# Low halves of split weights: an accumulating DMA in place of a VectorE subtraction

## The chip, the cores and the metric

The kernel runs on one core of a Trainium2 chip. The metric is device time in microseconds (us) of one execution. The engines are TensorE (PE; PEld is its weight load), VectorE (DVE), ScalarE (ACT), GpSimd (POOL) and SyncE (SP). Each works through its own instructions in order; they wait for each other and for DMAs through semaphores.

## The reference

One decoder layer on a 1024 x 1024 float32 input. Behind a projection to seven parts stand two token mixers in parallel and an output projection:

```python
h = rms_norm(x, pre_g)
conv_in, z_c, u_s, z_s, g_c, g_s = split(h @ w_in)
ca, cb = split(conv_in)
cu = silu(layer_norm(causal_depthwise_conv(ca * sigmoid(cb), conv_w, conv_b)))
conv_out = (cu * silu(z_c)) @ w_conv_out
y = gelu(s5_mimo(u_s, ...))                      # complex-diagonal state, 32 groups
y = y * sigmoid(y @ w_glu + b_glu)
ssm_out = (y * silu(z_s)) @ w_ssm_out
merged = sigmoid(g_c) * conv_out + sigmoid(g_s) * ssm_out
out = x + rms_norm(merged @ w_out, post_g)
```

## The kernel before

**Three passes for each product.** TensorE works on a rounded format (fp32r). To keep float32 precision, both factors of a product are split into a high half, the rounded value, and a low half, the value minus its high half. A product then has three passes: high weight with high data, high weight with low data, low weight with high data. The weights of one output tile of 128 channels are a *unit*: a 128 x 1024 tile for the products of depth 1024 (cb, ca, gc, zc, gs, zs, co, and us), and 128 x 512 for those of depth 512 (glu, so). A unit of depth 1024 has 8 slices k, each with three passes of two matmuls of 512 columns, 48 matmuls; a unit of depth 512 has 24. The units follow each other in a list, `seq`: first us3, then pairs of cb and ca with gc and zc between them, the four glu, the zs, the alternating gs and so, and at the end the eight co. Then comes the output product, `po`, whose weights (wo) are split too.

**How a weight comes to TensorE.** SP loads the raw tile of a unit (`wr_`, L706). ACT copies it to the rounded high half (`wh_`, L716, in `wsplit_h`). DVE subtracts the high half from the raw tile and writes the low half (`wl_`, L724, in `wsplit_l`). Raw, high and low tiles have two buffers each. During the product of one unit the next unit is split. After the low half is made, `wload` asks for the raw tile of the unit two further on, into the raw buffer that has just been read. That load therefore waits on SP's queue until the raw tile has been read, and what SP is to issue later waits behind it.

**Where the split stands in the program.** `product` issues the matmuls slice by slice. For a unit of depth 1024 it calls `flush` after slice 1, which issues the eviction of the product before (ACT or DVE reads the PSUM tile), `wsplit_h` after slice 2 and `wsplit_l` after slice 4. For a unit of depth 512 the places are slice 0, slice 0 and slice 2. The buffers, not these places alone, decide when the split can run: the high and low tile of unit u+1 use the buffers of unit u-1, and are free when TensorE has finished with u-1.

**Other work.** The S5 mixer (parameters, then four quarters), the depthwise convolution (some 350 multiply-adds on DVE, L551) and the layer norm are generators. `clk.tick` places their instructions between the matmuls, by a running model of when DVE is free; `clk.fg` adds to it what other work costs DVE. POOL has little: sums of squares at the start, powers in small pieces for the S5 parameters (L234), a memset in each S5 quarter (L462), and powers for the norms. SP issues all DMAs.

Of the kernel before, what the change touches and what calls it, by code (L numbers as in the profile page):

```python
# [10 lines left out]
AF = mybir.ActivationFunctionType  # L11
ALU = mybir.AluOpType
# [23 lines left out]
def tile_hybrid_block(  # L36
# [25 lines left out]
    V, A, G, PE = nc.vector, nc.scalar, nc.gpsimd, nc.tensor  # L62
# [17 lines left out]
    def PS(name, tag):  # L80
        return ps.tile([128, 1024], F32, tag=tag, name=name)

    def f32(t):
        return t.bitcast(F32)
# [599 lines left out]
    clk = Clock()  # L684
# [6 lines left out]
    def wsrc(kind, m):  # L691
        base = {"cb": M_CB, "ca": M_CA, "gc": M_GC, "gs": M_GS, "zc": M_ZC, "zs": M_ZS, "us": M_US}
        if kind in base:
            return w_in[base[kind] + m], 8
        return {"glu": (w_glu, 4), "so": (w_so, 4), "co": (w_co, 8), "wo": (w_out, 8)}[kind][0][m], \
            {"glu": 4, "so": 4, "co": 8, "wo": 8}[kind]
# [3 lines left out]
    def wload():  # L700
        if rnext[0] < len(order):
            u = order[rnext[0]]
            rnext[0] += 1
            src, kt = wsrc(*u)
            raw = wp.tile([128, 1024], F32, tag="wraw", name=f"wr_{u[0]}{u[1]}", bufs=WRAW)
            nc.sync.dma_start(out=raw[:, 0:kt * 128], in_=src)  # L706
            raws[u] = (raw, kt)

    def wsplit_h():
        if wnext[0] < len(order):  # L710
            u = order[wnext[0]]
            wnext[0] += 1
            raw, kt = raws.pop(u)
            n = kt * 128
            h = wp.tile([128, 1024], F32R, tag="wh", name=f"wh_{u[0]}{u[1]}", bufs=WHL)
            A.activation(out=h[:, 0:n], in_=raw[:, 0:n], func=AF.Copy)  # L716
            half[0] = (u, raw, h, n)

    def wsplit_l():
        if half[0]:  # L720
            u, raw, h, n = half[0]
            half[0] = None
            l = wp.tile([128, 1024], F32R, tag="wl", name=f"wl_{u[0]}{u[1]}", bufs=WHL)
            V.tensor_tensor(out=l[:, 0:n], in0=raw[:, 0:n], in1=f32(h[:, 0:n]), op=ALU.subtract)  # L724
            clk.fg(1.14 * n / 1024)
            wt[u] = (h, l)
            wload()

# [5 lines left out]
    def flush():  # L734
        while posts:
            posts.pop(0)()

    def js(j):
        return slice(j * 512, (j + 1) * 512)

    def product(name, u, rh, rl, tag="mm"):
        p = PS(name, tag)
        h, l = wt.pop(u)
        kt = wsrc(*u)[1]
        for k in range(kt):
            ks = slice(k * 128, (k + 1) * 128)
            for lhs, rhs, st, sp_ in ((h, rh, k == 0, False), (h, rl, False, False), (l, rh, False, k == kt - 1)):
                for j in range(2):
                    PE.matmul(p[:, js(j)], lhsT=lhs[:, ks], rhs=rhs(k, j), start=st, stop=sp_)  # L749
            if kt == 4 and k == 0:  # L750
                wsplit_h()
            if k == (1 if kt == 8 else 0):
                flush()
            if kt == 8 and k == 2:
                wsplit_h()
            if k == (4 if kt == 8 else 2):
                wsplit_l()
            clk.tick(1.296)
        return p

    def proj(u, tag="mm"):
        return product(f"p{u[0]}{u[1]}", u, lambda k, j: xh[:, k, js(j)], lambda k, j: xl[:, k, js(j)], tag)
# [55 lines left out]
    for k in range(8):  # L818
# [19 lines left out]
        h, l = wus[k // 2]  # L838
# [3 lines left out]
        for n_, (m, i) in enumerate([(m, i) for i in range(3) for m in range(3)]):  # L842
            lhs, rhs = passes[i]
            for j in range(2):
                js_ = slice(j * 512, (j + 1) * 512)
                PE.matmul(usp[m][:, js_], lhsT=lhs[:, kk[m]], rhs=rhs[:, k, js_], start=(k == 0 and i == 0),
                          stop=(k == 7 and i == 2))
            if n_ == 4:
                if k == 4:
                    x_sums(rb)  # L850
                if k == 5:
                    rbc = x_spread(rb)
                    clk.dve = max(clk.dve, clk.now + 1.5)
                    clk.add('s5', s5_chain())
                for k_ in {6: (0, 1), 7: (2, 3)}.get(k, ()):
                    x_norm(k_, rbc)
                if k == 7:
                    wsplit_h()
                    wsplit_l()
            clk.tick(0.45)  # L860
# [25 lines left out]
    for u in seq:  # L886
# [29 lines left out]
        elif kind == "yhl":  # L916
            clk.until('s5', lambda: s5_done[0])
            continue
        elif kind == "glu":
            p = product(f"pgl{m}", u, lambda k, j: yh[k][:, js(j)], lambda k, j: yl[k][:, js(j)])  # L920

            def f(p=p, m=m):
# [16 lines left out]
        elif kind == "gs":  # L939
            p = proj(u)  # L940

            def f(p=p, m=m):
                sgs[m] = T(f"gst{m}")
                A.activation(out=sgs[m], in_=p, func=AF.Sigmoid)  # L944
        elif kind == "so":
            p = product(f"pso{m}", u, lambda k, j: y2h[k][:, js(j)], lambda k, j: y2l[k][:, js(j)])

            def f(p=p, m=m):
# [43 lines left out]
    for k in range(8):  # L992
        if k < WHL:
            if ("wo", k) not in wt:
                wsplit_h()
                wsplit_l()
            woh[k], wol[k] = wt[("wo", k)]
        else:
            raw = wp.tile([128, 1024], F32, tag="wraw", name=f"wor{k}", bufs=WRAW)
            nc.sync.dma_start(out=raw, in_=w_out[k])  # L1000
            woh[k], wol[k] = xw[0][:, k, :], xw[1][:, k, :]
            split(woh[k], wol[k], raw)
# [134 lines left out]
```

## Time and profile before

| | us |
|---|---|
| median of 3 runs | 856.16 |
| lowest and highest of the runs | 855.4, 856.76 |
| the profiled execution, its own time | 855.18 |
| its span in the profile | 853.1 |
| PE busy | 826.1 |
| DVE busy | 630.6 |
| ACT busy | 279.3 |
| POOL busy | 45.9 |

The mean granted TensorE clock of the profiled execution was 0.992. How to read the rows: a row of the timeline gives the start, the length, the engine, the line, the operation, what is written and read, the shape, how many instructions were merged, and in brackets the idle time of the engine just before with what ended it. In a row of the groups the two numbers after the bar are the busy time in us and the mean of one instruction in ns. In a row of a DMA the last number is the median time from issue to landing. The ends of matmuls are modelled.

### The profile page before, as it was taken

What the parts mean: (1) busy time and instruction counts of PE and PEld (TensorE: products, weight loads), DVE (VectorE), ACT (ScalarE), POOL (GpSimd) and SP (SyncE); (2) the same over time, 40 slices, a digit from 0 to 9 for tenths busy, and PEclk for the clock granted to TensorE, in tenths of its full rate; (3) what the DMA queues carried; (4) which work ended last, traced back from release to release, by engine and by line L of the source; (5) the groups of instructions that cost most, each with busy time, mean ns of one, the idle gap of its engine ahead of it and who ended that gap; (6) DMA issues with size and microseconds to landing.
All of it is one profiled execution on the core that took longest, in us unless ns stands there. A gap on an engine that the chain in (4) does not pass through costs nothing.

```text
span 853.1 us, 9817 instructions
## 1 busy us (share of the span) xinstructions
PE 826.1 (97%) x3888; PEld 685.6 (80%) x3888; DVE 630.6 (74%) x902; ACT 279.3 (33%) x292; POOL 45.9 (5%) x32
## 2 busy tenths in 40 slices
PE   6898999999999999999999999999999999999996
PEld 5776778888888888888888888888878788888885
DVE  5576699989989988999998959589594544452242
ACT  7233155253344426333222221133252411122121
POOL 3660000000000000000000000000000000000010
PEclk9799999999999999999999999999999999999999
DMA  9103433233231321211111212212253343325142
GB/s 336 51 25 123 149 99 107 80 90 123 91 83 66 110 75 50 75 49 50 50 38 62 87 38 99 74 61 85 103 210 135 117 184 142 142 85 195 49 173 98
DMA packets 34028, 86.58 MB, mean 101 GB/s; under 512 B 8176, under 2 KB 12912, under 8 KB 33984
## 3 DMA queue, kind: packets, MB, share of 16 engines
q1 hardware_dynamic: 33984, 85.97, 29.5%
q8 instruction: 30, 0.49, 0.2%
q14 instruction: 14, 0.11, 0.0%
HBM read 61.71 MB, written 18.87 MB: 94 GB/s over the span
## 4 chain that ended last, share of the span: by engine, by line
PE 81%; DVE 6%; issue 1%; ACT 1%; DMA 1%; SPq 1%; DVEq 0%; POOLq 0%; ACTq 0%
PE pco L749 10%; PE po L1010 10%; PE pgs L749 9%; PE pgc L749 9%; PE pca L749 9%; PE pzc L749 9%; PE pcb L749 9%; PE pzs L749 5%; PE pso L749 4%; PE pgl L749 2%; PE yp L504 1%; PE yp L503 1%; PE ep L425 1%; PE lnp L589 1%; SPq L204 1%
## 5 line engine op out<-in xcount | busy, mean ns | idle before, releaser
L551 DVE SCALAR_TENSOR_TENSOR pp<-ext,cw,pp 128x512 f32<-128x512 f32 x232 | 165.0, 744 | 7.6 <-ACT pp L542 7.6
L551 DVE SCALAR_TENSOR_TENSOR acc<-ext,hs,acc 128x512 f32<-128x512 f32 x120 | 89.3, 744 | 0.0
L1010 PE MATMUL po<-wox,mgh 128*128 128x512 f32 x192 | 52.3, 389 | 0.0
L749 PE MATMUL pcb<-xh,wh_cb 128*128 128x512 f32 x128 | 40.2, 395 | 2.3 <-ACT wh_cb L716 2.3
L1010 PEld LDWEIGHTS po<-wox,mgh 128*128 128x128 f32 x192 | 36.0, 188 | 7.5
L1026 DVE TENSOR_TENSOR o<-po,postg 128x1024 f32<-128x1024 f32 (+1 forms) x9 | 10.0, 1106 | 42.0 <-ACT q L1025 42.0
L749 PE MATMUL pcb<-xh,wl_cb 128*128 128x512 f32 x128 | 39.7, 391 | 1.4 <-DVE wl_cb L724 1.3
L749 PE MATMUL pco<-cuh,wl_co 128*128 128x512 f32 x128 | 39.5, 390 | 1.3 <-DVE wl_co L724 1.3
L749 PE MATMUL pgs<-xh,wh_gs 128*128 128x512 f32 x128 | 39.6, 391 | 1.0 <-ACT gst L944 1.0
L749 PE MATMUL pgc<-xh,wh_gc 128*128 128x512 f32 x128 | 40.2, 395 | 0.0
L749 PE MATMUL pzc<-xh,wh_zc 128*128 128x512 f32 x128 | 40.0, 394 | 0.0
L749 PE MATMUL pca<-xh,wh_ca 128*128 128x512 f32 x128 | 39.8, 392 | 0.0
L749 PE MATMUL pgs<-xh,wl_gs 128*128 128x512 f32 x128 | 39.5, 390 | 0.0
L749 PE MATMUL pgc<-xl,wh_gc 128*128 128x512 f32 x128 | 39.5, 389 | 0.0
L749 PE MATMUL pzc<-xl,wh_zc 128*128 128x512 f32 x128 | 39.5, 389 | 0.0
L749 PE MATMUL pco<-cuh,wh_co 128*128 128x512 f32 x128 | 39.4, 389 | 0.0
L749 PE MATMUL pgc<-xh,wl_gc 128*128 128x512 f32 x128 | 39.4, 389 | 0.0
L749 PE MATMUL pca<-xh,wl_ca 128*128 128x512 f32 x128 | 39.4, 389 | 0.0
L749 PE MATMUL pcb<-xl,wh_cb 128*128 128x512 f32 x128 | 39.4, 389 | 0.0
L749 PE MATMUL pco<-cul,wh_co 128*128 128x512 f32 x128 | 39.4, 389 | 0.0
L749 PE MATMUL pzc<-xh,wl_zc 128*128 128x512 f32 x128 | 39.4, 389 | 0.0
L749 PE MATMUL pca<-xl,wh_ca 128*128 128x512 f32 x128 | 39.4, 389 | 0.0
(270 smaller groups left out, 1784.3 us busy)
## 6 DMA issues: line engine op xcount, KB each, us to landing
xt<-in_xt_dram SPq DMA_DIRECT2D x8, 512.0 KB, 6.1
wr_cb<-in_w_in_dram SPq DMA_DIRECT2D x8, 512.0 KB, 3.2
wr_ca<-in_w_in_dram SPq DMA_DIRECT2D x8, 512.0 KB, 3.3
wr_gc<-in_w_in_dram SPq DMA_DIRECT2D x8, 512.0 KB, 3.5
gc_scratch<-gct SPq DMA_DIRECT2D x8, 512.0 KB, 3.3
wr_zc<-in_w_in_dram SPq DMA_DIRECT2D x8, 512.0 KB, 3.2
zc_scratch<-zct SPq DMA_DIRECT2D x8, 512.0 KB, 2.6
wr_gs<-in_w_in_dram SPq DMA_DIRECT2D x8, 512.0 KB, 3.2
```

The source lines that it names most:

```text
L204: nc.sync.dma_start(out=usU[m][16 * (7 - t):16 * (8 - t)].rearrange("p (g n) -> p g n", g=8), in_=src[t])
L425: pe(lambda g, s: PE.matmul(epp[:, s], lhsT=R[:, s], rhs=U[:, s], start=True, stop=True), 1.8)
L503: PE.matmul(yp[:, s], lhsT=U[:, s], rhs=Mt[:, s], start=True, stop=False)
L504: PE.matmul(yp[:, s], lhsT=Sx[:, s], rhs=O1[:, s], start=False, stop=True)
L551: V.scalar_tensor_tensor(out=o, in0=src(e, r), scalar=w, in1=o, op0=ALU.mult, op1=ALU.add)
L589: PE.transpose(p[:, t * 128:(t + 1) * 128], acc[c][:, t * 128:(t + 1) * 128], ident)
L749: PE.matmul(p[:, js(j)], lhsT=lhs[:, ks], rhs=rhs(k, j), start=st, stop=sp_)
L1010: PE.matmul(p[:, js(j)], lhsT=lhs[k][:, s], rhs=rhs[k][:, js(j)], start=st, stop=sp_)
L1026: V.tensor_tensor(out=o[:, s], in0=p, in1=pog[:, s], op=ALU.mult)
```

## The change

The subtraction on DVE is gone. In its place ACT copies the high half once more, with scale -1, into the low tile, and POOL issues a DMA that reads the raw tile and adds it to the low tile in place: minus high plus raw. The model's charge for DVE goes with it. And both halves are now split after slice 0 of a product, whatever its depth; the next raw load stands there too, ahead of the eviction of the product before.

```diff
             l = wp.tile([128, 1024], F32R, tag="wl", name=f"wl_{u[0]}{u[1]}", bufs=WHL)
-            V.tensor_tensor(out=l[:, 0:n], in0=raw[:, 0:n], in1=f32(h[:, 0:n]), op=ALU.subtract)
-            clk.fg(1.14 * n / 1024)
+            A.activation(out=l[:, 0:n], in_=f32(h[:, 0:n]), func=AF.Copy, scale=-1.0)
+            G.dma_start(out=l[:, 0:n], in_=raw[:, 0:n], accum_op=ALU.add)
             wt[u] = (h, l)
             wload()
...
                 for j in range(2):
                     PE.matmul(p[:, js(j)], lhsT=lhs[:, ks], rhs=rhs(k, j), start=st, stop=sp_)
-            if kt == 4 and k == 0:
+            if k == 0:
                 wsplit_h()
+                wsplit_l()
             if k == (1 if kt == 8 else 0):
                 flush()
-            if kt == 8 and k == 2:
-                wsplit_h()
-            if k == (4 if kt == 8 else 2):
-                wsplit_l()
             clk.tick(1.296)
```

Three places of the order are shown. The first is POOL's queue, from the square root of the mean squares (r8t) over the powers of the S5 parameters (spt) to the first memset of an S5 quarter (Mt). Before:

```order
L165 TENSOR_TENSOR r8t_98<-ssq8_97,mhalf_86 128x8
L234 TENSOR_TENSOR spt1_341<-spar_339,lamt_90 128x8 x4
L234 TENSOR_TENSOR spt4_384<-spar_339,spt3_382 128x8 x4
L462 MEMSET Mt0_966 128x1024
L462 MEMSET Mt1_1369 128x1024
```

And with the change:

```order
L234 TENSOR_TENSOR spt1_341<-spar_339,lamt_90 128x8 x4
L234 TENSOR_TENSOR spt4_384<-spar_339,spt3_382 128x8
L725 DMA wl_us3_396<-wr_us3_309 128x1024
L725 DMA wl_cb0_467<-wr_cb0_311 128x1024
L725 DMA wl_ca0_523<-wr_ca0_399 128x1024
L234 TENSOR_TENSOR spt4_384<-spar_339,spt3_382 128x8 x3
L725 DMA wl_gc0_640<-wr_gc0_470 128x1024
L725 DMA wl_cb1_765<-wr_cb1_526 128x1024
L725 DMA wl_ca1_857<-wr_ca1_643 128x1024
L462 MEMSET Mt0_936 128x1024
```

POOL now issues an accumulating DMA for each unit, in line with its other work; three of the four pieces of the second power stand behind the DMAs of us3, cb0 and ca0.

The second place is ACT's queue where gs and so alternate: the unit gs1 is split during the product of so0 (gst0 is the eviction of gs0, ext5, pp5 and acc5 belong to the convolution). Before:

```order
L527 ACTIVATE ext5_3321<-ext5_3321 128x3x3x131
L716 ACTIVATE wh_so0_3332<-wr_so0_3179 128x512
L542 ACTIVATE pp5_3335<-ext5_3321,cw_82 128x512
L543 ACTIVATE pp5_3335<-ext5_3321,nb1_84,cw_82 128x512
L544 ACTIVATE acc5_3334<-ext5_3321,hs_83 128x4x128
L716 ACTIVATE wh_gs1_3390<-wr_gs1_3251 128x1024
L944 ACTIVATE gst0_3392<-pgs0_3308 128x1024
L716 ACTIVATE wh_so1_3445<-wr_so1_3356 128x512
```

And with the change:

```order
L716 ACTIVATE wh_so0_3349<-wr_so0_3201 128x512
L724 ACTIVATE wl_so0_3351<-wh_so0_3349 128x512
L527 ACTIVATE ext5_3362<-ext5_3362 128x3x3x131
L542 ACTIVATE pp5_3374<-ext5_3362,cw_82 128x512
L543 ACTIVATE pp5_3374<-ext5_3362,nb1_84,cw_82 128x512
L544 ACTIVATE acc5_3373<-ext5_3362,hs_83 128x4x128
L716 ACTIVATE wh_gs1_3425<-wr_gs1_3279 128x1024
L724 ACTIVATE wl_gs1_3427<-wh_gs1_3425 128x1024
L941 ACTIVATE gst0_3432<-pgs0_3342 128x1024
L716 ACTIVATE wh_so1_3467<-wr_so1_3354 128x512
L724 ACTIVATE wl_so1_3469<-wh_so1_3467 128x512
```

Each high half is now followed by the negated copy of it, and the split of so0 has moved ahead of the wait for ext5.

The third place is ACT's queue at the passage from the last co product to the output product (mgh6 and mgh7 are high halves of the merged data, wo0 and wo1 the first two weight tiles of the output). Before:

```order
L874 ACTIVATE mgh6_5275<-sgr6_5191 128x1024
L716 ACTIVATE wh_wo0_5285<-wr_wo0_5171 128x1024
L874 ACTIVATE mgh7_5321<-sgr7_5256 128x1024
L716 ACTIVATE wh_wo1_5327<-wr_wo1_5236 128x1024
L874 ACTIVATE wox0_5325<-wor2_5331 128x1024
```

And with the change:

```order
L716 ACTIVATE wh_wo0_5332<-wr_wo0_5205 128x1024
L724 ACTIVATE wl_wo0_5334<-wh_wo0_5332 128x1024
L871 ACTIVATE mgh6_5345<-sgr6_5255 128x1024
L871 ACTIVATE mgh7_5387<-sgr7_5321 128x1024
L716 ACTIVATE wh_wo1_5393<-wr_wo1_5271 128x1024
L724 ACTIVATE wl_wo1_5395<-wh_wo1_5393 128x1024
```

The split of wo0 has moved ahead of mgh6; that of wo1 is still behind mgh7, and has the negated copy behind it.

## The prediction

> **What bounds the kernel now.** First the busy times and the chain that ended last, from the profile's page:
>
> ```profile
> PE 826.1 (97%) x3888; PEld 685.6 (80%) x3888; DVE 630.6 (74%) x902; ACT 279.3 (33%) x292; POOL 45.9 (5%) x32
> PE 81%; DVE 6%; issue 1%; ACT 1%; DMA 1%; SPq 1%; DVEq 0%; POOLq 0%; ACTq 0%
> ```
>
> TensorE is the bound. VectorE, which the change relieves, works 74% of the span beside it, so what it is relieved of shortens the time only where TensorE stands still for it. Those places are in TensorE's timeline: rows with an idle time in brackets, from the start of the us3 product on.
>
> ```profile
> 56.95 0.74 PE L749 MATMUL pus<-xh,wh_us 128*128 128x512 f32 x2 [0.96 <-ACT wh_us L716]
> 65.19 0.73 PE L749 MATMUL pus<-xl,wh_us 128*128 128x512 f32 x2 [0.35 <-DVE xl L179]
> 67.52 0.73 PE L749 MATMUL pus<-xl,wh_us 128*128 128x512 f32 x2 [0.67 <-DVE xl L179]
> 69.79 0.74 PE L749 MATMUL pus<-xl,wh_us 128*128 128x512 f32 x2 [0.63 <-DVE xl L179]
> 73.19 0.73 PE L749 MATMUL pcb<-xh,wl_cb 128*128 128x512 f32 x2 [1.29 <-DVE wl_cb L724]
> 107.55 0.73 PE L749 MATMUL pcb<-xh,wh_cb 128*128 128x512 f32 x2 [2.27 <-ACT wh_cb L716]
> ...
> 338.33 0.73 PE L749 MATMUL pgl<-yh,wl_glu 128*128 128x512 f32 x2 [0.20 <-DVE wl_glu L724]
> ...
> 637.12 0.73 PE L749 MATMUL pgs<-xh,wh_gs 128*128 128x512 f32 x2 [0.96 <-ACT gst L944]
> ...
> 672.29 0.74 PE L749 MATMUL pco<-cuh,wl_co 128*128 128x512 f32 x2 [1.33 <-DVE wl_co L724]
> ...
> 764.83 0.74 PE L1010 MATMUL po<-wl_wo,mgh 128*128 128x512 f32 x2 [0.17 <-DVE wl_wo L724]
> ```
>
> Each stop costs about 0.3 more than its bracket, since modelled ends overlap the next start and the next pair comes late too. The nine stops that the change can touch (all but the first) come to 7.9 + 9 x 0.3 = 10.6 us. That is all there is to win, 1.2% of the time.
>
> **What it removes and adds.** The groups of instructions give the prices:
>
> ```profile
> L724 DVE TENSOR_TENSOR wl_gs<-wr_gs,wh_gs 128x1024 fp32r<-128x1024 f32 x8 | 9.7, 1217 | 4.2 <-ACT wh_gs L716 4.2
> L716 ACT ACTIVATE wh_gs<-wr_gs 128x1024 fp32r<-128x1024 f32 x8 | 8.4, 1055 | 11.7 <-issue 8.1 <-PE pgs L749 3.6
> L724 DVE TENSOR_TENSOR wl_so<-wr_so,wh_so 128x512 fp32r<-128x512 f32 x8 | 5.5, 684 | 0.0
> L716 ACT ACTIVATE wh_so<-wr_so 128x512 fp32r<-128x512 f32 x8 | 5.0, 624 | 8.9 <-issue 6.9 <-PE pso L749 2.0
> ```
>
> The 55 units of 1024 columns and 12 of 512 lose 55 x 1.22 + 12 x 0.68 = 75 us on VectorE. ACT gains 55 x 1.05 + 12 x 0.62 = 65 us and would be at 344 of 853. Neither sum is on the path. What is on it is the delay of the split: 1.05 + 1.22 us before; now 1.05 + 1.0 for two copies in a row, and then the accumulating DMA. Call D the time from the end of the negated copy until TensorE can use the low half.
>
> **The price D.** No DMA here is issued by POOL and none adds. The nearest rows are a copy of 512 KB within SBUF in two halves (Zw), from SP's queue and VectorE's timeline; loads of 512 and 256 KB; and POOL's instructions:
>
> ```profile
> 143.24 0.51 SPq L488 DMA_DIRECT2D Zw<-Zs  x1
> 143.79 0.59 SPq L489 DMA_DIRECT2D Zw<-Zs  x1
> ...
> 147.81 1.23 DVE L396 TENSOR_TENSOR Zw<-Zw,tk 128x1024 f32<-128x1024 f32 x1 [0.40 <-DMA Zw<-Zs]
> ```
>
> ```profile
> wr_gs<-in_w_in_dram SPq DMA_DIRECT2D x8, 512.0 KB, 3.2
> wr_so<-in_w_so_dram SPq DMA_DIRECT2D x8, 256.0 KB, 2.6
> ```
>
> ```profile
> L234 POOL TENSOR_TENSOR spt<-spar,spt 128x8 f32<-128x8 f32 x4 | 8.3, 2100 | 3.5 <-DVE spt L224 3.5
> ```
>
> Zw was used 147.81 - 143.24 = 4.6 us after its issue, and VectorE was waiting for it. An accumulating DMA also reads its destination, another 512 KB; from 256 to 512 KB a load grows by 0.6, so 1.2 more. That gives 5.8. One of Zw's two issues falls away, and POOL's issue stands in its place. Lower bound: 3.2, a plain load. Upper bound: 5.8 and one of POOL's slow instructions, 2.1, so 7.9. I take **D = 5.8**, since Zw stays inside SBUF as this does. The Trainium skill (DMA: Bandwidth & Descriptors, Anatomy of one DMA) fits 2.0 us + bytes / 436 GB/s for POOL's DMAs, an estimate of 3.2 us, at which the sum below would be 2.6 us of gain. Against it speaks the skill's Collectives: The Full Stack (The bandwidth ceiling): an add in the DMA reads two sources through one ring and moves at half the rate. That makes the estimate 4.4 and the sum a loss of 2 us; no row here shows an add.
>
> **Where D is hidden.** The split of unit u+1 can begin when TensorE leaves unit u-1; the low half is first needed by the third pair of unit u+1. Here gs1 is split under so0, in ACT's and TensorE's timelines:
>
> ```profile
> 455.16 1.07 ACT L716 ACTIVATE wh_gs<-wr_gs 128x1024 fp32r<-128x1024 f32 x1 [3.24 <-issue]
> ```
>
> ```profile
> 455.37 0.62 PE L749 MATMUL pso<-y2h,wh_so 128*128 128x512 f32 x2
> 460.81 0.62 PE L749 MATMUL pgs<-xh,wh_gs 128*128 128x512 f32 x2
> 461.83 0.73 PE L749 MATMUL pgs<-xh,wl_gs 128*128 128x512 f32 x2
> ```
>
> The 12 pairs of so0 take 5.44 us, 0.453 each; a unit of depth 1024 takes 10.88. The high copy starts 0.2 before so0, both copies are done at 455.16 + 2.05 = 457.2, and without a stop the third pair comes at 460.81 + 0.91 = 461.7. So D up to **4.5** is hidden under a short product, and up to 4.5 + 5.4 = 9.9 under a long one. Long products hide 5.8; a 512-wide split under a short product (two copies of 0.62, so 5.3 left, against 5.8 - 0.6) is just hidden too. Nine splits of 1024 columns lie under a short one: behind glu3 and so0 to so7. Each costs 5.8 - 4.5 = 1.3: **+11.7 us**. Two of them have ACT late besides:
>
> ```profile
> 632.53 1.25 ACT L635 ACTIVATE acc<-acc,chn 128x1024 f32<-128x1024 f32 x1 [2.28 <-DVE acc L634]
> 633.69 1.04 ACT L716 ACTIVATE wh_gs<-wr_gs 128x1024 fp32r<-128x1024 f32 x1
> 664.65 1.03 ACT L944 ACTIVATE gst<-pgs 128x1024 f32<-128x1024 f32 x1 [10.70 <-PE pgs L749]
> 665.58 1.05 ACT L716 ACTIVATE wh_co<-wr_co 128x1024 fp32r<-128x1024 f32 x1
> ```
>
> In the layer norm the high copy was 3.3 behind its earliest start (637.12 - 0.96 - 5.44 - 0.35, about 630.4); 1.9 of that were subtractions on VectorE that go, so 1.4 stay. For co0 the eviction gst is first, 1.3. Together +2.7, less the stops that stood there (637.12 and 672.29: 1.3 + 1.6): **-0.2**. At the glu the copies of y come one product earlier now, and the stop at 338.33 goes: **-0.5**.
>
> **The start.** Nothing lies ahead of us3 to hide its split:
>
> ```profile
> 56.93 1.23 DVE L724 TENSOR_TENSOR wl_us<-wr_us,wh_us 128x1024 fp32r<-128x1024 f32 x1 [0.99 <-ACT wh_us L716]
> 58.20 0.73 PE L749 MATMUL pus<-xh,wl_us 128*128 128x512 f32 x2
> 88.56 0.38 SPq L706 DMA_DIRECT2D wr_gc<-in_w_in_dram  x1
> 92.64 1.06 ACT L716 ACTIVATE wh_gc<-wr_gc 128x1024 fp32r<-128x1024 f32 x1 [6.09 <-DMA wr_gc<-in_w_in_dram]
> 95.10 0.64 PE L749 MATMUL pgc<-xh,wl_gc 128*128 128x512 f32 x2
> ```
>
> ACT ends the high copy at 56.9 and the negated one at 57.9, so the third pair moves from 58.20 to 57.9 + D: D - 0.3 late. The three stops for xl (2.6) and the one at 73.19 (1.6) vanish in that: D - 4.5 = +1.3. VectorE, without 0.99 + 1.23 of waiting and subtracting, runs 2.2 ahead, and with it the chain of us stores and loads on SP's queue up to the load of gc0: its raw tile comes at 90.4, both copies end at 92.5, the low half at 98.3. It is needed at 95.10 + 1.3: +1.9. The stop at 107.55 goes (2.6), because ACT now splits cb1 ahead of the wait for VectorE's ext. Sum D - 5.2 = **+0.6**. The three powers that now stand on POOL behind ca0's DMA (6.2 us) delay the S5 parameters to about the time at which TensorE wants the first transposes; I cost this at nothing, with VectorE's 2.2 as cover, and at up to 3 if that is gone.
>
> **The end.** The split of wo1 stands behind the last high half of the merged data:
>
> ```profile
> 761.32 1.06 ACT L874 ACTIVATE mgh<-sgr 128x1024 fp32r<-128x1024 f32 x1 [8.87 <-DVE sgr L983]
> 762.28 1.04 ACT L716 ACTIVATE wh_wo<-wr_wo 128x1024 fp32r<-128x1024 f32 x1
> ```
>
> Its copies end at 762.28 + 2.0 = 764.3, its low half comes at 770.1 and was used at 764.83: **+5.3**.
>
> The next raw load waits for the DMA instead of the subtraction: about 2.0 + 5.8 + 3.2 = 11 us into a product, wanted two products on, at 16.3 at the earliest. Hidden. Evictions stand 2 us further back on ACT; TensorE wants their buffer a product later. Hidden.
>
> **Sum.** 11.7 - 0.2 - 0.5 + 0.6 + 5.3 = +16.9, on the profiled execution's 855.18 (its span 853.1 and 2.1 around it): 872.1. The median is 1.0 above it: **873**. Each us of D above 4.5 is worth 11 (nine splits, start, end); below it about 2.
>
> **Rivals.** *A DMA as quick as a plain load (not slower).* Place: the same nine splits. At D = 3.2 start -2.0, glu -0.5, end +2.7, layer norm and co0 together -2.8: -2.6, so 853.6. It decides below D = 3.9, where the sum is nought. For it: 3.2 is what 512 KB from HBM take, with landing. Against: Zw took 4.6 without an add. Chance 18% for D under 4.4. *A DMA slower than a long product hides.* At D = 10 the nine cost 49.5, the ends 4.8 + 9.5, the three 512-wide splits under glu 4 each, some forty long ones 0.1 to 0.3: about 80, so 935; from D = 7.9 on (46, so 902) this is its region. For it: POOL's pieces of 8 columns take 2.1 us. Chance 12%. *SP's queue takes over.* The load behind the accumulating DMA blocks SP up to 7.8 us into each product, and the swap Zw stands behind it. A late Zw stops VectorE, then Sx, then TensorE's yp:
>
> ```profile
> 149.07 1.22 DVE L497 TENSOR_TENSOR Sx<-Et,Zw 128x1016 f32<-128x1016 f32 x1
> ```
>
> ```profile
> 155.77 0.22 PE yp L503 x2
> ```
>
> Sx was done 5.5 us ahead of yp, so a block of 7.8 costs 2.3 in each of four quarters: 9, so 882. Against: VectorE, relieved, brings Zs sooner. Chance 8%.
>
> **How the numbers follow.** Forecast, D from 4.4 to 7.9: 62%; the rivals 18, 12 and 8. The range 854 to 900 runs from the quick DMA to the upper bound of D and leaves about 20% out. A measurement here can tell about 0.2%, 1.7 us, from no change. Faster by more needs D under 3.5: 8%. Within it, 3.5 to 4.4: 10%. Slower: 82%.
>
> **What would show it.** Right: stops of TensorE at the third pair of us3, gc0, of each 1024-wide unit behind a short one, and at the second k of the output, all put down to the DMA of a wl tile; long products following each other without a stop. D is read there. Wrong: no stop behind so (D under 4.5), stops behind long products too (D over 9.9), or stops at yp or rp.

## The result and the profile after

| | before | after |
|---|---|---|
| median, us | 855.97 | 896.33 |
| lowest and highest, us | 855.4, 856.76 | 896.17, 899.31 |
| span of the profiled execution, us | 853.1 | 893.5 |
| mean granted TensorE clock | 0.992 | 0.976 |

The changed kernel takes 1.0479 times as long, 95% interval 1.0456 to 1.0503: 40 us more, where 17 were forecast. The direction and the range held; the size did not. The busy times of the profile after, and the shares of the chain that ended last:

```profile
PE 840.2 (94%) x3888; PEld 694.1 (78%) x3888; DVE 562.8 (63%) x835; ACT 344.1 (39%) x357; POOL 103.2 (12%) x99
PE 46%; issue 22%; DMA 12%; DVE 11%; POOL 3%; ACT 3%; SPq 2%; POOLq 0%; DVEq 0%; ACTq 0%
```

ACT gained 65 us of busy time, as worked out beforehand. VectorE is busy 68 us less, not 75: the subtractions did last 75 us added up, but in part beside their neighbours. TensorE, with the same 3888 matmuls, is busy 14 us longer: some of them ran slower. TensorE's timeline after the change shows where it stood still and which matmuls were slow:

```profile
63.48 1.22 PE L749 MATMUL pus<-xh,wl_us 128*128 128x512 f32 x2 [4.91 <-DMA wl_us<-wr_us]
64.50 1.05 PE L749 MATMUL pus<-xh,wh_us 128*128 128x512 f32 x2
65.36 1.05 PE L749 MATMUL pus<-xl,wh_us 128*128 128x512 f32 x2
...
102.10 0.74 PE L749 MATMUL pgc<-xh,wl_gc 128*128 128x512 f32 x2 [2.04 <-DMA wl_gc<-wr_gc]
...
206.16 0.49 PE L504 MATMUL yp<-O,Sx 128*128 128x128 f32 x2 [1.39 <-DVE Sx L497]
...
221.71 1.06 PE L413 MATMUL rp<-ident,RT 128*128 128x128 f32 x8 [1.51 <-DVE RT L410]
...
340.48 0.33 PE L589 MATMUL lnp<-ident,acc 128*128 128x128 f32 x1 [3.46 <-DVE acc L559]
...
454.70 0.35 PE L589 MATMUL lnp<-ident,acc 128*128 128x128 f32 x1 [3.44 <-DVE acc L559]
...
484.74 0.72 PE L749 MATMUL pgs<-xh,wl_gs 128*128 128x512 f32 x2 [0.25 <-DMA wl_gs<-wr_gs]
...
666.65 1.22 PE L749 MATMUL pgs<-xh,wh_gs 128*128 128x512 f32 x2 [4.76 <-ACT gst L941]
...
706.23 0.74 PE L749 MATMUL pco<-cuh,wl_co 128*128 128x512 f32 x2 [1.66 <-DMA wl_co<-wr_co]
...
803.53 1.22 PE L1007 MATMUL po<-wl_wo,mgh 128*128 128x512 f32 x2 [4.94 <-DMA wl_wo<-wr_wo]
```

Only some of these stops are put down to the DMA. Those at yp (the output product of an S5 quarter), rp (transposes for S5) and lnp (transposes of a finished channel of the convolution, for the layer norm), where the kernel before had none, wait for VectorE, the engine that was relieved; the one at 666.65 waits for an eviction on ACT. The rows at 64.50 and 65.36 start 0.86 apart where a pair takes 0.453: for some us after a long stop TensorE works at about half speed, and its granted clock from 62.35 to 69.17 is 0.50. Taking the same product's start in both timelines, the added time arises like this:

| up to the start of | before | after | late by |
|---|---|---|---|
| second gc product | 134.77 | 140.55 | 5.8 |
| first zs (behind S5 and glu) | 354.77 | 372.11 | 17.3 |
| first gs | 444.39 | 467.11 | 22.7 |
| gs5, ahead of the stop at the layer norm | 619.67 | 644.34 | 24.7 |
| so6, behind that stop | 648.13 | 681.16 | 33.0 |
| output product | 758.60 | 792.54 | 33.9 |
| end of the span | 853.1 | 893.5 | 40.4 |

The price D can now be read: the negated copy, POOL's issue and the first use of gs1's low half (the row at 484.74), and the DMAs with their median times from issue to landing:

```profile
478.83 1.07 ACT L724 ACTIVATE wl_gs<-wh_gs 128x1024 fp32r<-128x1024 f32 x1
480.19 0.86 POOL L725 DMA_DIRECT2D wl_gs<-wr_gs  x1 [10.89 <-ACT wl_gs L724]
```

```profile
wl_gs<-wr_gs POOLq DMA_DIRECT2D x8, 512.0 KB, 4.5
wl_so<-wr_so POOLq DMA_DIRECT2D x8, 256.0 KB, 4.7
wl_glu<-wr_glu POOLq DMA_DIRECT2D x4, 256.0 KB, 3.3
Zw<-Zs SPq DMA_DIRECT2D x8, 256.0 KB, 5.7
zcr<-zc_scratch SPq DMA_DIRECT2D x8, 512.0 KB, 6.3
...
zc_scratch<-zct SPq DMA_DIRECT2D x8, 512.0 KB, 5.0
```

From the end of the copy at 479.90 to 484.74 are 4.8 us, where 5.8 was taken. Behind a short product this leaves a stop of 0.25. Half the bytes land in 3.3 (glu); those of so, between 3.3 and 8.1, land no sooner in the median (4.7). The swap Zw, the load zcr and the store zc_scratch take longer than before (3.7, 4.9 and 2.6).

### The profile page after: what moved, and what is told of

Read it like the earlier page. It is cut to its first block, busy times and chain, and to the rows that moved or that the text cites. A ratio compares the mean times of both kernels' runs of the same rounds, so it can differ in the third digit from the quotient of the medians.

```text
span 893.5 us, 9985 instructions
## 1 busy us (share of the span) xinstructions
PE 840.2 (94%) x3888; PEld 694.1 (78%) x3888; DVE 562.8 (63%) x835; ACT 344.1 (39%) x357; POOL 103.2 (12%) x99
## 4 chain that ended last, share of the span: by engine, by line
PE 46%; issue 22%; DMA 12%; DVE 11%; POOL 3%; ACT 3%; SPq 2%; POOLq 0%; DVEq 0%; ACTq 0%
PE pco L749 10%; PE po L1007 9%; PE pzc L749 6%; PE pgc L749 5%; PE pca L749 4%; PE pcb L749 4%; PE pgs L749 2%; DVE pp L551 2%; DMA wl_gs<-wr_gs 2%; POOL sq L157 2%; PE pgl L749 2%; SPq L204 1%; DMA Zw<-Zs 1%; DMA us_scratch<-usT 1%; DVE acc L551 1%
## 5 line engine op out<-in xcount | busy, mean ns | idle before, releaser
L749 PE MATMUL pgs<-xl,wh_gs 128*128 128x512 f32 x128 | 40.3, 397 | 0.0
L523 DVE TENSOR_TENSOR ext<-pca,sg 128x1024 f32<-128x1024 f32 x8 | 9.6, 1205 | 48.1 <-PE pca L749 48.1
```

Of the source, the lines that this page charges most:

```text
L523: V.tensor_tensor(out=ext[:, 0:2, 3:7, 4:132], in0=pa.rearrange("p (i e n) -> p e i n", i=4, e=2), in1=sg.rearrange("p (i e n) -> p e i n" ...
```

## Experiments

Each run is timed beside the kernel before, whose median was 855.6 to 856.0 throughout.

### Three parts taken apart: charge, place, DMA

**e1, the charge put back.**

```diff
             G.dma_start(out=l[:, 0:n], in_=raw[:, 0:n], accum_op=ALU.add)
+            clk.fg(1.14 * n / 1024)
```

> The changed kernel with the model's charge of 1.14 us per 1024 columns put back behind the accumulating DMA, so that VectorE's work is placed between the matmuls nearly as before. Nothing else differs. Theory ORDER (without the charge the model thinks VectorE free too early and places transposes, S5 steps and taps where VectorE has not got to them): the stops at rp, lnp and yp go, which are 1.7 + 1.4 + 3.6 + 3.6 us and the slow matmuls behind the last three, about 14 together: about 882. Theory QUEUE (SP's queue stands behind the accumulating DMAs, so the swaps Zw and E2 and the scratch loads come late): the stops stay, 894 to 898. Theory PRICE (the stops come from the time of the DMA at the third pair alone): 894 to 898 as well.

887.72 us, ratio 1.0373 (1.0352 to 1.0394). The stops at 340.48 and 454.70 and those at rp and yp are gone: from the second gc to the first gs TensorE now loses 1.6 us against the kernel before, where the changed kernel loses 16.9. ORDER holds there. But the start is 5.5 dearer than in the changed kernel (11.3 against 5.8), since three of the S5 powers now stand on POOL behind the DMA of gc0 and not of ca0. VectorE's wait for them, in the changed kernel and in e1:

```profile
DVE spt L237 <- POOL spt L234: 14.0, 1, 14.0
```

```profile
DVE spt L237 <- POOL spt L234: 33.3, 1, 33.3
```

So the whole gain is 8.6 us, not 14, and 887.72 lies between the times of ORDER and those of the other two.

**e2, the early place alone, with VectorE's subtraction.**

```diff
-            if kt == 4 and k == 0:
+            if k == 0:
                 wsplit_h()
+                wsplit_l()
...
-            if kt == 8 and k == 2:
-                wsplit_h()
-            if k == (4 if kt == 8 else 2):
-                wsplit_l()
```

> The kernel before with only the place of the split changed: both halves behind slice 0, low half still by VectorE with its charge. Theory ORDER, QUEUE and PRICE all: no DMA is added, so no new long stop; the stop of 2.6 us at the second cb and the 1.3 us at the layer norm go, 851 to 856. A rival PLACE (the early split takes ACT and VectorE away from evictions and S5 work): above 858, with stops at rp, yp or lnp as in the changed kernel.

869.47 us, 1.0157 (1.0137 to 1.0177): the rival PLACE. VectorE's waits in this kernel (us in all, times, longest) and TensorE's timeline show why:

```profile
DVE wl_gc L724 <- ACT wh_gc L716: 25.4, 5, 19.8
DVE wl_so L724 <- ACT wh_so L716: 15.4, 5, 6.7
```

```profile
118.29 0.44 PE L413 MATMUL rp<-ident,RT 128*128 128x128 f32 x2 [2.34 <-DVE RT L410]
...
200.40 0.30 PE L589 MATMUL lnp<-ident,acc 128*128 128x128 f32 x1 [3.31 <-DVE acc L559]
```

The subtraction stands so early in VectorE's queue that it waits for ACT's high copy, and with it all that is queued behind. In the changed kernel there is no subtraction on VectorE, so this loss cannot be its own; e7 below, early as well and without subtraction or DMA, loses 1.4.

**e3 and e7, no DMA, without and with the charge.**

```diff
             A.activation(out=l[:, 0:n], in_=f32(h[:, 0:n]), func=AF.Copy, scale=-1.0)
-            G.dma_start(out=l[:, 0:n], in_=raw[:, 0:n], accum_op=ALU.add)
+            clk.fg(1.14 * n / 1024)       # e7 only
```

> The changed kernel without the accumulating DMA: the low tile holds minus the high half only, so the raw weight is missing from the third pass. Copies on ACT, model and placement stay. PRICE and QUEUE: all the added time hangs on the DMA, so 850 to 857. ORDER: the stops at rp, lnp and yp stay (about 14 us), the rest goes: 864 to 872.

> The changed kernel without the accumulating DMA (the third pass has minus the high half only) and with the model's charge put back; placement stays early. Theory ORDER: the 10 us that were left without the DMA were the missing charge, so 854 to 858. Rival, the early split on ACT costs them: 863 to 867.

866.10 (1.0114, 1.0089 to 1.0139) and 857.17 (1.0017, 1.0001 to 1.0032). Without the DMA, 10 us are still lost, and the charge takes 9 of them back. TensorE's timeline of e3 has the two stops at lnp as long as in the changed kernel:

```profile
331.66 0.33 PE L589 MATMUL lnp<-ident,acc 128*128 128x128 f32 x1 [3.45 <-DVE acc L559]
...
445.28 0.47 PE L589 MATMUL lnp<-ident,acc 128*128 128x128 f32 x1 [3.44 <-DVE acc L559]
```

The waits of VectorE for the ca product at the gate of the convolution are, in the order before, changed, e3, e7:

```profile
DVE ext L523 <- PE pca L749: 13.4, 2, 6.7
```

```profile
DVE ext L523 <- PE pca L749: 48.1, 4, 14.2
```

```profile
DVE ext L523 <- PE pca L748: 48.0, 4, 14.2
```

```profile
DVE ext L523 <- PE pca L749: 14.8, 3, 6.5
```

They go with the charge and not with the DMA. Without the charge the model lets VectorE run out of convolution work: it stands at the next gate for up to 14 us, and the transposes of the channel that follows are placed ahead of the moment when VectorE has finished with it. Why the model errs by just so much is not shown. e1 against e7, both with the charge, leaves 887.72 - 857.17 = **30.5 us** for the DMA; e7 against before leaves 1.4 for the early place and the added ACT copies together.

**e5, DMA and charge at the old places.** The two replaced lines alone, on the kernel before.

```diff
-            V.tensor_tensor(out=l[:, 0:n], in0=raw[:, 0:n], in1=f32(h[:, 0:n]), op=ALU.subtract)
+            A.activation(out=l[:, 0:n], in_=f32(h[:, 0:n]), func=AF.Copy, scale=-1.0)
+            G.dma_start(out=l[:, 0:n], in_=raw[:, 0:n], accum_op=ALU.add)
```

> The kernel before with only the subtraction replaced by the negated copy and the accumulating DMA; the split stays behind slices 2 and 4 (0 and 2 in short products) and the model's charge stays. Theory PLACE (the early split by itself costs 14, as it did with VectorE's subtraction): 887.7 less 14, about 874. Rival: with the DMA the place costs nothing, since what waited early in that run was VectorE's subtraction for ACT's high copy, and here there is none: 884 to 891.

908.87 us, 1.0619 (1.0596 to 1.0642): both expectations missed. TensorE now stops at third pairs that the early split had covered:

```profile
147.83 0.80 PE L750 MATMUL pgc<-xh,wl_gc 128*128 128x512 f32 x1 [4.36 <-DMA wl_gc<-wr_gc]
...
674.93 0.80 PE L750 MATMUL pgs<-xh,wl_gs 128*128 128x512 f32 x1 [3.94 <-DMA wl_gs<-wr_gs]
```

So the early place costs 14 us with the subtraction and saves 21 with the DMA. The effects of the parts do not add.

### What the DMA's 30 us are made of

**e4, low-weight passes last, on the changed kernel.**

```diff
+        pairs_ = [(h, f_, i) for i in range(kt) for f_ in (rh, rl)] + [(l, rh, i) for i in range(kt)]
         for k in range(kt):
-            for lhs, rhs, st, sp_ in ((h, rh, k == 0, False), (h, rl, False, False), (l, rh, False, k == kt - 1)):
+            for n_, (w_, f_, i) in enumerate(pairs_[3 * k:3 * k + 3]):
```

> The changed kernel with the passes of a product in another order: high weight with high and low data for all slices first, low weight for all slices last. The low half is wanted at the 17th pair of a long product in place of the 3rd, 6.3 us later, and at the 9th in place of the 3rd of a short one, 2.7 us later. Places in the program are the same. PRICE: the stops at us3 (5.1 and some 2.8 of slow matmuls), gc0 (2.2 and 1.6) and behind the short products (6 of 0.5), and at co0 (1.8) go, about 16 us: 880. ORDER or QUEUE as the main cause: the stops at rp, yp, lnp, the layer norm and the output stay, and with them some 24 us over the kernel before.

889.27 us, 1.0391 (1.0370 to 1.0412): 7 us, not 16. The stops at us3, gc0's third pair, behind short products and at co0 are gone. But us3 now asks for xl, the data's low halves, sooner and stops there three times (0.75, 1.14 and 1.08), and gc0 stops for 4.4 ahead of its first pair, waiting for the eviction sg on ACT.

**e12, a plain DMA by POOL in place of the adding one.**

```diff
-            G.dma_start(out=l[:, 0:n], in_=raw[:, 0:n], accum_op=ALU.add)
+            G.dma_start(out=f32(l[:, 0:n]), in_=raw[:, 0:n])
+            clk.fg(1.14 * n / 1024)
```

> The changed kernel with the charge put back (887.7) and a plain DMA by POOL in place of the accumulating one: the low tile then holds the raw weight, the high half is not taken from it. It tells what the adding costs. If a DMA that adds is slower because it reads two sources, landing falls from 4.5 to 3.2 to 3.8, the stops at the third pair of us3 and at the second weight of the output fall from 5.1 to some 4, and the time to 879 to 884. If the landing is set by POOL's issue and the fixed part of a DMA, it stays within 0.3 of 4.5 and the time within 886 to 890.

876.78 us, 1.0238 (1.0213 to 1.0263), 10.9 less than e1. Its DMAs:

```profile
wl_gs<-wr_gs POOLq DMA_DIRECT2D x8, 512.0 KB, 2.9
...
wl_so<-wr_so POOLq DMA_DIRECT2D x8, 256.0 KB, 2.3
```

Landing and time came out below both expectations. The adding itself costs 1.6 us of landing for 512 KB, since the same DMAs in e1 took 4.5. For 256 KB it costs 1.0, by the glu tiles, which land in 3.3 in e1 and 2.3 here; the so tiles (4.1 in e1) spread from 3.3 to 6.0 there. And a DMA that lands in 2.9, quicker than in the rival of the quick DMA, still leaves the kernel 21 us slower than before. In the profiled execution, whose span is 24.0 longer, 9.5 are lost by the second gc, 8.6 at the layer norm and 6.6 from the output's start on. The price of the DMA was not where the forecast's error lay. The Trainium skill (Collectives: The Full Stack, The bandwidth ceiling) says of the reduce step of a collective that its add reads two sources and moves at half the rate; with the fit of the skill's DMA: Bandwidth & Descriptors (Anatomy of one DMA) that made the estimates 4.4 with the add and 3.2 without. The measured 4.5 and 2.9 agree well for 512 KB. For 256 KB the same working gives an estimate of 3.2, and the glu tiles took 3.3.

**e6, e9, e11, the next raw load asked for one product later**, so that it does not stand on SP's queue behind a DMA under way: everywhere on the changed kernel (e6), everywhere with the charge (e9), and with the charge from the twelfth unit on (e11).

```diff
     def wsplit_h():
         if wnext[0] < len(order):
+            if wnext[0] >= 12:            # e11; e6 and e9: from the second unit on
+                wload()
...
             wt[u] = (h, l)
-            wload()
+            if wnext[0] < 12:             # e6 and e9: never here
+                wload()
```

> The changed kernel with one thing moved: the load of the next raw tile is asked for one product later, just ahead of the next split, so that on SP's queue it never stands waiting for an accumulating DMA that is still under way. Theory QUEUE: the waits of VectorE for zcr (6.0 and more) and for Zw (10.7 in all) shrink, the stop of 4.9 at the layer norm with 3.5 behind it and the one at yp go: 884 to 888. If the transfers are late because the DMA rings are busier and not because of SP's order: 893 to 897.

> The changed kernel with the charge put back and the raw load asked for one product later. ORDER and QUEUE together: what is left is the price of the DMA where nothing hides it (us3 5.1 and 2.8 slow, gc0 2.4, behind short products 0.6 each, co0 1.8, wo1 5.1 and 1.5): 873 to 879. If QUEUE is wrong: 886 to 889.

> The changed kernel with the charge put back (887.7), and the raw load asked for one product later from the twelfth unit on; the start, where a later load itself came too late, is left as it was. Theory QUEUE, as far as the last pair of runs leaves it: Zw and zcr come in time, the stop of 1.1 at the fourth lnp goes and the one at the layer norm shrinks by 2.8: 883 to 885. If SP's queue is no cause at all: 887 to 889.

901.16 (1.0534, 1.0508 to 1.0560), 887.63 (1.0372, 1.0349 to 1.0394), 883.39 (1.0311, 1.0288 to 1.0334). In e6 VectorE's waits for Zw fall from 10.7 to 3.8 and those for zcr from 7.1 to 0.4, so SP's queue did cause them. Yet e6 got slower, above both expectations: the raw tile of ca0 itself was now late (ACT waited 24 us for it), and TensorE stopped in that product for 5.5 and 5.3. e9 has the same two stops (7.1 and 5.3) and is no faster than e1, which by its expectation would say that QUEUE is wrong; but what it gains later it loses at the start, where it is some 3.5 dearer than e1. e11, which leaves the start alone, gains 4.3 on e1: VectorE's waits for Zw fall from 9.8 to 1.8 and those for zcr from 16.5 to 7.4. The mechanism at the layer norm, in the timelines of POOL and SP, then of VectorE, ACT and TensorE, in e1:

```profile
640.39 0.92 POOL L725 DMA_DIRECT2D wl_so<-wr_so  x1 [15.07 <-ACT wl_so L724]
643.75 0.33 SPq L706 DMA_DIRECT2D wr_so<-in_w_so_dram  x1
644.65 1.97 SPq L603 DMA_DIRECT2D zcr<-zc_scratch  x3
```

```profile
650.27 1.23 DVE L628 TENSOR_TENSOR acc<-acc,zcr 128x1024 f32<-128x1024 f32 x1 [5.59 <-DMA zcr<-zc_scratch]
653.92 1.24 ACT L635 ACTIVATE acc<-acc,chn 128x1024 f32<-128x1024 f32 x1 [7.96 <-DVE acc L634]
659.58 1.22 PE L750 MATMUL pgs<-xh,wh_gs 128*128 128x512 f32 x2 [8.04 <-ACT gst L942]
```

The raw load waits on SP for the accumulating DMA, zcr stands behind it, and VectorE stands still for zcr. ACT waits for VectorE, then makes the two copies of the split and only then the eviction gst, and TensorE waits for gst.

### The DMA hidden

**e10, everything so far on one kernel:** e4, the charge, e11's load, us3's passes with all high data first, and in the output product the low pass of the second weight behind the third weight.

```diff
+        if u[0] == "us":
+            pairs_ = [(h, rh, i) for i in range(8)] + [(h, rl, i) for i in range(4)]
+            pairs_ += [(l, rh, i) for i in range(8)] + [(h, rl, i) for i in range(4, 8)]
...
-    for k in range(8):
+    for k, ii in [(0, (0, 1, 2)), (1, (0, 2)), (2, (0, 1, 2)), (1, (1,))] + [(k, (0, 1, 2)) for k in range(3, 8)]:
         for t in range(4):
-            out_k(pt[t], t, k)
+            out_k(pt[t], t, k, ii=ii)
```

> The changed kernel with all that the runs so far point to: the charge; the raw load asked for later from the twelfth unit on; low-weight passes last in each product (in us3 behind the first twelve pairs); in the output product the low pass of the second weight behind the third weight. The accumulating DMA is then hidden everywhere. PRICE: the stops at us3, gc0, behind short products, at co0 and at the output go with their slow matmuls, 887.7 less 7.3, 3, 4, 2 and 7, less 4 for the queue: 858 to 864. If the added transfers cost time in another way (rings, the raw chain at the start), 868 or more.

871.94 us, 1.0179 (1.0158 to 1.0199): in the branch that says time is lost in another way. No stop is put down to an accumulating DMA any more. 12 us were lost by the second gc: us3 stopped for high data that came late (0.88, 1.66 and 1.36), and then the second cb stopped:

```profile
118.52 0.77 PE L757 MATMUL pcb<-xh,wh_cb 128*128 128x512 f32 x1 [5.13 <-DVE ext L523]
```

VectorE was late there after a wait of 33 us for the powers, as in e1.

**e13 and e14, the powers ahead of the DMAs on POOL's queue**, on the changed kernel and on e11.

```diff
                 G.tensor_tensor(out=r[:, g_], in0=ebase2[:, g_], in1=a[:, g_], op=ALU.pow)
-                yield 0.0, 1.6
+            yield 0.0, 6.4
```

> The changed kernel with one thing moved: the four pieces of each power of the S5 parameters are issued to POOL together, so that all of them stand ahead of the first accumulating DMA on POOL's queue. Theory POOLQ (three of them stood behind the DMA of ca0 and VectorE waited 14.0 us for them; what was late then cost TensorE): VectorE's wait goes, and the time falls by 2 to 6, to 890 to 894. If that wait lay beside other slack: 895 to 898.

> The same move of the powers on the kernel with the charge and the later raw load (883.4), where the three pieces stood behind the DMA of gc0 and VectorE waited 33 us. POOLQ: the stops of 1.2 at the second cb and of 1.5 at rp go, 878 to 881. Otherwise 882 to 885.

898.84 (1.0501, 1.0475 to 1.0528) and 883.49 (1.0321, 1.0292 to 1.0349): no gain in either. The DMA of us3 now waits for POOL, and TensorE for the DMA, as POOL's and TensorE's timelines of e13 show:

```profile
50.03 9.62 POOL L234 TENSOR_TENSOR spt<-spar,spt 128x8 f32<-128x8 f32 x4 [3.51 <-DVE spt L224]
59.61 1.05 POOL L725 DMA_DIRECT2D wl_us<-wr_us  x1
```

```profile
64.74 0.80 PE L749 MATMUL pus<-xh,wl_us 128*128 128x512 f32 x1 [7.91 <-DMA wl_us<-wr_us]
```

The stop of 4.9 at us3 became one of 7.9. And VectorE's wait only moved: in e14 it waits for the sines that ACT makes of the powers. Its wait and ACT's timeline:

```profile
DVE PR L224 <- ACT spar L295: 29.2, 1, 29.2
```

```profile
97.28 1.06 ACT L718 ACTIVATE wh_gc<-wr_gc 128x1024 fp32r<-128x1024 f32 x1 [15.63 <-DMA wr_gc<-in_w_in_dram]
...
100.74 1.02 ACT L895 ACTIVATE sg<-pcb 128x1024 f32<-128x1024 f32 x1
...
103.08 0.23 ACT L291 ACTIVATE spar<-spar 128x32 f32<-128x32 f32 x1
```

In the kernel before, the eviction sg and the sines stood ahead of gc0's high copy and ran at 83.51 and 85.84. With the split behind slice 0 the high copy is first, waits for a raw tile that SP issues only behind the loads of U, the input of S5, and holds back sg, for which TensorE waits ahead of gc0, and the sines. e7 has that stop too, without any DMA by POOL (4.87).

**e15, the repaired kernel mended; e16, VectorE's subtraction kept for the start and the output.** e15 is e10 with the powers ahead, plain low-last in us3, and in short products the eviction ahead of the split. e16:

```diff
+    def by_dve(u):
+        return u[0] in ("us", "wo") or u in (("cb", 0), ("ca", 0), ("gc", 0), ("cb", 1), ("ca", 1))
...
+            if by_dve(u):
+                V.tensor_tensor(out=l[:, 0:n], in0=raw[:, 0:n], in1=f32(h[:, 0:n]), op=ALU.subtract)
+            else:
+                A.activation(out=l[:, 0:n], in_=f32(h[:, 0:n]), func=AF.Copy, scale=-1.0)
+                G.dma_start(out=l[:, 0:n], in_=raw[:, 0:n], accum_op=ALU.add)
```

> The repaired kernel (871.9) with three mends: the powers together ahead of the DMAs; in us3 the low-weight passes simply last, since asking for all high data first stopped TensorE five times; in short products the eviction ahead of the split on ACT. POOLQ: the 5.3 at the second cb go; us3 gains some 4; the stop of 5.0 at the layer norm with its slow matmuls loses 2 or more: 858 to 864. If what is left hangs on the added transfers themselves: 867 or more.

> Subtraction on VectorE, placed as before, for the units of the start (us3, cb0, ca0, gc0, cb1, ca1) and for wo; negated copy and accumulating DMA for all others, with the charge, the raw load later, the split behind slice 0 and low-weight passes last. Where the DMA is fully hidden it should cost nothing and gain nothing: 852 to 858. If the transfers, or the two copies on ACT, cost time by themselves: 862 or more.

862.80 (1.0083, 1.0057 to 1.0110) and 855.63 (1.0004, 0.9990 to 1.0019). e15 keeps two long stops, 6.7 for sg ahead of gc0 and 3.5 at the layer norm, neither of them for a DMA by POOL. e16 is level with the kernel before, with 59 of the 67 splits by DMA, and VectorE has 58 us less to do:

```profile
PE 829.1 (97%) x3888; PEld 687.3 (80%) x3888; DVE 572.3 (67%) x843; ACT 338.2 (40%) x351; POOL 97.4 (11%) x91
```

Hidden, the accumulating DMA costs nothing that can be told here, and relieving an engine that TensorE seldom waits for gains nothing. e16 has the low-weight passes last too; on the kernel before these alone make no change that can be told (e8, below).

### A version that beats both

**e8 and e17, subtraction on VectorE with the stops of the kernel before taken away.** e8: low-weight passes last in all products but us3. e17 also:

```diff
             if kt == 4 and k == 0:
+                flush()
                 wsplit_h()
+            if name == "pgc0" and k == 0:
+                wsplit_h()
...
-            if kt == 8 and k == 2:
+            if kt == 8 and k == 2 and name != "pgc0":
                 wsplit_h()
```

> The kernel before, subtraction on VectorE, with the low-weight passes last in each product but us3. The stops at the first cb (1.6 with what follows), the glu (0.5) and co0 (1.6) go: 851 to 853. If the data's low halves, now wanted sooner, stop TensorE instead: 856 or more.

> The kernel before, subtraction on VectorE, with what the stops point to: low-weight passes last in each product but us3; the high copy of the second cb ahead of the wait for ext on ACT; in short products the eviction ahead of the high copy. If TensorE's stops are all there is to win, the ones at the first cb (1.6), the second cb (2.6), the glu (0.5), the layer norm (1.3) and co0 (1.6) go: 848 to 851. If the evictions and halves that move cause other stops: 853 or more.

855.51 (0.9987, 0.9973 to 1.0001), no change that can be told, and 853.31 (0.9977, 0.9965 to 0.9989), faster by 0.1 to 0.35%, though not the 5 to 8 us expected. In e17 the stops at the first and second cb are gone, and two others have come, in TensorE's timeline:

```profile
94.05 0.73 PE L752 MATMUL pgc<-xh,wh_gc 128*128 128x512 f32 x2 [1.21 <-ACT wh_gc L716]
...
112.50 1.09 PE L413 MATMUL rp<-ident,RT 128*128 128x128 f32 x8 [1.76 <-DVE RT L410]
```

In this kernel a stop at the start that is taken away is mostly paid at the next late thing.

## Why the prediction was right and wrong

The forecast was 17 us more, and 40 came. In the sum's own terms: the charge stood at nothing and costs 8.6; the start stood at +0.6 and costs 5.8; the layer norm with co0 stood at -0.2, and the layer norm alone costs 8.4. The nine splits stood at 11.7 and cost about 0.6 each, some 6 too much, which by luck hid part of what the other terms lacked.

**Right: D and where it is hidden.** D is 4.8, inside 3.2 to 7.9. Up to 4.5 hides under a short product, and the stop behind one was 0.25. Long products follow each other without a stop for the DMA. But 1 us of D mattered: the nine splits behind short products, the largest term at 11.7, cost about 0.6 each where their stop stands free (e1 less e7: seven steps, 4.0). The mis-sized part of D is its base, "Zw was used 147.81 - 143.24 = 4.6 us after its issue". The plain DMA of e12 lands in 2.9, and at us3 its third pair comes 3.4 after the end of the copy where e1 takes 5.1. The 1.2 taken for the adding measured 1.6.

**Right in the stop, wrong in its price: us3 and the output.** Counted from the start of its product, the third pair of us3 came 4.9 later than before (D - 0.3 gave 5.5) and the second wo 4.8 (5.3). The step "each stop costs about 0.3 more than its bracket" failed: it was read from stops of 0.2 to 2.3 us behind which the clock stayed full, and does not hold where it falls to half. Those two were followed by 2.8 and 1.5 us of slow pairs, which no term had. In the table the passage from the output's start to the end is 6.5 dearer, not 5.3.

**Wrong: the charge.** "The model's charge for DVE goes with it" stands under the change, and no step of the sum priced it. From the second gc to the first gs, where the sum had -0.5 for the glu, 16.9 us were lost, the largest part of the miss; with the charge back, 1.6. Moved instructions were costed only where the split itself moved; that the same model sets the places of TensorE's transposes and VectorE's taps was left out. The sign named for being wrong, "stops at yp or rp", came.

**Partly wrong: SP's queue.** As a rival it had 8% and 882. It is real, at Zw as described and at zcr, which was not seen; but what e11 won back is 4.3 us of 40, not the bound; what it costs at the start, where a later load came too late, was not separated. "The next raw load waits ... Hidden" was true of the raw tile and not of what stands behind it on SP.

**Wrong: the layer norm and co0, -0.2.** Up to the so behind the layer norm alone it was +8.4. Two steps failed. "1.9 of that were subtractions on VectorE that go, so 1.4 stay": without subtraction and DMA (e7) the high copy began at 634.79, no sooner than before (633.69), since VectorE came to the norm 1.1 later and then waited 1.69 for zcr. And "Evictions stand 2 us further back on ACT; TensorE wants their buffer a product later. Hidden.": here TensorE waited for the eviction gst already before (0.96), and in e7 gst begins at 638.23 where it began at 636.04. So without any DMA for the low halves the stage already loses 4.0 behind gst, a stop of 3.44 and the slow pairs that follow. With DMA and charge it is 9.2 (e1), and 6.1 with the raw load later (e11), so SP's queue has 3 of it. At co0 the eviction that stands first, put at 1.3, and the 0.3 that D leaves give 1.6, and the stop was 1.66: right.

**Wrong: the start, +0.6.** It was 5.8. The slow pairs behind us3 and gc0 are 2.8 and 1.8 of it. "I cost this at nothing", of the powers on POOL, had VectorE's 2.2 as cover where VectorE waited 14.0. And "ACT now splits cb1 ahead of the wait for VectorE's ext" saw the gain of the early place on ACT and not its loss, gc0's split ahead of sg and the sines. What each of the two costs alone stays open: when one is mended, VectorE waits for the other.

The sum in one line: 40.4 (40.5 by the parts) = 8.6 charge + 30.5 DMA + 1.4 ACT copies and early place, of the DMA 4.3 by SP's queue from the twelfth unit on. By places the 30.5 are, e1 against e7, 10.8 at the start, 1.4 in S5, 4.0 behind short products, 5.3 at the layer norm, 2.0 at co0 and about 7 at the output.

## What to carry to other kernels

When a change takes work off an engine, look for every place where its cost was written down as well: a planner's charge decides where other engines' work stands, and taking it out can cost as much as the change itself. A wait that is put on a queue has to be priced for all that stands behind it on that queue, on SP, ACT and POOL alike, and the price of an edit should be taken together with its place, since the same move cost 14 us with one way of splitting and saved 21 with the other. Price a stop of the bound engine by its length and by what its clock does behind it: here short ones cost little more than themselves, and those above 3.4 us cost about 2.3 more.

## What the hardware showed unexpectedly

**The clock after a stop.** The slow pairs, 0.85 to 1.02 where 0.453 is usual, go with the granted clock. In the changed kernel it is 0.50 from 62.35 to 69.17 (behind the stop at us3), 103.31 to 106.72 (gc0), 342.24 to 345.65 and 454.88 to 458.30 (lnp), 666.51 to 673.33 (layer norm) and 803.04 to 806.45 (output), and 1.00 between them; in the kernel before it is 1.00 from 41.55 to 850.50. Each stretch is 3.41 us long or twice that, and they begin whole multiples of 3.41 apart. A stop then costs, behind it, half of what is left of the stretch: (69.17 - 63.48) / 2 = 2.8 at us3 and (806.45 - 803.53) / 2 = 1.5 at the output, as measured. Whether a stretch follows is told by the window of 3.41 ahead of it. In rows of the changed kernel's trace the numbers are the window, its length, TensorE's busy time (by modelled ends), its instructions, the granted clock, the share of the DMA engines and their GB/s:

```profile
99.90:103.31 3.41, 1.37 (x6) 1.00 1.13 163
103.31:106.72 3.41, 3.41 (x10) 0.50 1.18 207
...
335.42:338.83 3.41, 1.61 (x8) 1.00 0.53 98
338.83:342.24 3.41, 1.49 (x10) 1.00 0.57 210
342.24:345.65 3.41, 3.41 (x10) 0.50 0.00 0
```

With 1.61 busy the next window had the full clock, with 1.49 and with 1.37 half of it. Over the traces of all 19 kernels, from us3 to 10 us before the end, the 69 windows at full clock that were idle for 56% or more were all followed by one at half clock, and none of those idle for 55% or less was. So the place of a stop counts beside its length. The 2.04 at gc0 lay in one window, 60% idle, and 1.8 us were lost behind it; the 2.27 at the second cb of the kernel before lay in two, 33% and 36% idle (from 102.99 and from 106.40), and the clock stayed at 1.00. Counting stops with no other of over 0.15 us in the 3 us ahead or the 9 us behind: behind 45 stops of 0.9 to 1.9 us the matmuls that follow lose 0.2 us on average (0.1 to 0.3), behind 36 of 3.4 us and more they lose 2.3 (1.5 to 3.3), and behind the 19 between anything from 0.1 to 3.0. The Trainium skill (TensorE: Matmul & The Clock Gate, Part 1) says that the clock falls to half after an idle window of about 3.4 us and comes back after as long a busy one, the windows running freely. The length of the windows agrees, as does the 0.86 for two matmuls of 512 columns, which it gives as 0.427 each. But the window did not have to be idle throughout: 56% was enough here.

**The accumulating DMA.** Its issue takes 0.86 us on POOL. By the gs and glu tiles it lands in 4.5 for 512 KB and 3.3 for 256 KB, the plain one of e12 in 2.9 and 2.3: the second 256 KB cost 1.2 with the add and 0.6 without. With other transfers under way it takes longer: in e11 the DMAs of the co tiles land in 8.8 in the median, where raw load and loads from scratch run beside them and the share of the DMA engines is 1.02 from 700 to 712. Other transfers are slower too: the stores to zc_scratch land in 5.0 where it was 2.6. That is not the adding, since with the plain DMA they take 5.0 as well; without any DMA by POOL (e3) they take 2.9, and with the raw load later (e11) 4.0. What SP's order and the shared DMA engines each have in it was not separated further.
